# Steps of gathers and combines at three fixed places of a chunk, five weight pieces apart

## The chip, the cores and the metric

The kernel runs on one core of a Trainium2 chip. The metric is the device time of one execution in microseconds (us), from the first to the last instruction with what the device needs around it; the time shown for a kernel is the median of its runs. Engines: PE (TensorE) multiplies matrices, DVE (VectorE) and ACT (ScalarE) work on rows of data, POOL (GpSimd) and SP (SyncE) do little here beyond issuing transfers.

## The reference

A trunk of two layers on 256 tokens of width 1024. Each layer mixes tokens (attention and a linear recurrence) and then channels. The first layer's channel mixer is dense. The second layer's is a mixture of eight experts, two for each token, and it is the part that the change touches:

```python
def swiglu(h, wg, wu, wd):
    return (jax.nn.silu(h @ wg) * (h @ wu)) @ wd

def moe_swiglu(h2, router, wg, wu, wd):
    ...
    logits = jnp.matmul(h2, router, preferred_element_type=jnp.float32)
    top_logit, top_e = lax.top_k(logits, TOP_K)
    top_w = jax.nn.softmax(top_logit, axis=-1)
    ...
    yb = lax.map(expert_block, (xg.reshape(n_blocks, MOE_BLOCK, d), block_e)).reshape(n_rows, d)
    return jnp.zeros_like(h2).at[tok_buf].add(yb * w_buf[:, None].astype(h2.dtype), mode='drop')
```

So the rows of an expert's tokens are gathered, go through gate (1024 to 3584), up (1024 to 3584) and down (3584 to 1024), are weighted, and are added back to their tokens. All weights are float32.

## The kernel before

**Arithmetic.** A float32 weight tile is split into a high part `wh` (ACT, line 121) and the remainder `wl` (DVE, line 124). With both operands in two parts a product takes three matmuls (lines 133 to 135). A *piece* is 128 x 1024 weights: one `wh` and one `wl`. Weights come in transfers of 2 MB, four pieces each, issued by SP into six slots.

**Experts.** Slot r = 0 holds expert 0, slots 1 to 7 the others in order of their token count. Slots 0 to 3 are *long* (128 rows), slots 4 to 7 *short* (64 rows; both parts of the activations stand side by side in one operand, so two matmuls a product do, lines 902 and 903). In a short expert about one piece in six is not split but multiplied whole in float32 (line 898).

**Steps.** The 3584 columns of an expert are cut into chunks of 512; a step `(r, f0, m)` takes m = 2 chunks, or 1 where 512 are left. Long and short steps alternate: `(0,0,1) (0,512,2) (4,0,2) (0,1536,2) (4,1024,2) (0,2560,2) (4,2048,2) (1,0,2) (4,3072,1) (1,1024,2) (5,0,2)` and so on to `(7,2048,2) (7,3072,1)`. The loop does gate (4m pieces), up (4m pieces), and then the down (`down`, 4 pieces for each chunk) of the step *before*. In the gate it also does that earlier step's `turn`: PE transposes its activations, ACT and DVE split them.

**Order.** `take()` hands out pieces and keeps five in hand, so the split of piece p+4 stands in the queues of ACT and DVE ahead of whatever the code writes after piece p. `keep_order` fixes the written order on PE, DVE and ACT. So what the code writes between two pieces stands just there on PE, and four pieces later among the splits on DVE and ACT.

**Side work.** `dispatch(r)` gathers the rows of slot r: a mask P and its weighted twin C on DVE (lines 842, 843), two halves of 24 small matmuls on PE (line 826) with their evacuation by ACT and DVE, and `places` (two transposes of C, reduced to `wp` and `PT`). `combine` adds a finished expert back, in two halves of 512 columns: `yh` on ACT (line 946), `yl` on DVE (line 947), four matmuls on PE (lines 951, 952), two additions to `xk` on DVE (line 953). Both are generators that wait in the list `behind`; a call of `advance()` runs the first of them to its next `yield`. Before the change `advance()` stands after every second piece in the gate (places 3 and 5, where the turns take 0 and 1) and after every second piece in the down. At the start of an expert the rest is done at once:

```python
            if f0 == 0:
                settle()
```

Such a start follows seven times: at slots 4 (nothing is left there), 1, 5, 2, 6, 3 and 7. At the last six a `combine` has been put into `behind` by the `down` just before, so that all of it is done there, between the last product of that down and the first product of the next gate.

**Banks.** PSUM has eight banks, four tags of two: y0 and y1 collect the downs of the long and the short expert, "g" the gate, "u" the up. Before the change turns, gathers and combines all use "u".

Of the kernel before, what the change touches and what calls it, by code (L numbers as in the profile page):

```python
# [10 lines left out]
F32 = mybir.dt.float32  # L11
# [22 lines left out]
NLONG, SHORT, LEAD = 3, 64, 2  # L34
# [25 lines left out]
def trunk_kernel(ctx: ExitStack, tc: tile.TileContext, x, positions, norm1_g, w_in, q_norm_g, w_uq,  # L60
# [702 lines left out]
    def moe(l, norm, lgT):  # L763
# [10 lines left out]

        def bank(tag="u"):
            t = banks.tile([128, 512], F32, name="bk", tag=tag, bufs=2)
            return t
# [51 lines left out]
        def dispatch(r):  # L829
# [15 lines left out]
            for j0 in range(0, DB, 4):  # L845
                pg = bank()
                gather(pg, j0, P)
                v = pg.rearrange("p (j s) -> p j s", j=4)
                js = slice(j0, j0 + 4)
                if sh:  # L850
                    if j0 == 0:
                        A.activation(xw, v[:, :, :SHORT], AF.Copy)
                    A.activation(xa[:, js, :SHORT], v[:, :, :SHORT], AF.Copy)
                    V.tensor_sub(xa[:, js, SHORT:], v[:, :, SHORT:], f32(xa[:, js, :SHORT]))
                else:
                    split_act(xgh[:, js], xgl[:, js], v)
                yield
            xg[r] = (xa, xw) if sh else (xgh, xgl)
# [80 lines left out]

        def combine(y, wp, PT):  # L940

            for n in range(2):
# [6 lines left out]
                for t in range(2):  # L949
# [3 lines left out]
                    V.tensor_add(xk[:, t, c], xk[:, t, c], po)  # L953
                yield

        behind = []

        def advance():

            if behind and next(behind[0], "end") == "end":  # L960
                behind.pop(0)

        def settle():
            while behind:
                advance()

# [14 lines left out]
        def overflow_round():  # L981
            en = mp.tile([128, 1], F32, name="en")
            V.memset(en, 0.0)
            with tc.For_i(0, NE, 1) as e:
# [21 lines left out]
                for f0 in chunks:  # L1006
# [18 lines left out]
                    for b in range(4):  # L1025
                        for n in range(2):
                            PE.matmul(y[n], at[:, b], w[:, b, n * 512:(n + 1) * 512],
                                      start=f0 == 0 and b == 0, stop=f0 + CH == FE and b == 3)
                behind.append(combine(y, *rows))
                settle()  # L1030
# [157 lines left out]
        def take():  # L1188
            while len(ready) < len(pieces):
                p = next(supplies, None)  # L1190
                if p is None:
                    break
                ready.append(p)
            return ready.pop(0)

        y = {}

        def down(r, f0, m, acts):
            sh = is_short(r)
            if f0 == 0:  # L1200
                y[sh] = [bank(f"y{int(sh)}") for _ in range(2)]
            for p in range(4 * m):
                pc = take()
                for n in range(2):
                    products(y[sh][n], acts, p, pc, 0, slice(n * 512, (n + 1) * 512), f0 == 0 and p == 0,
                             f0 + m * CH == FE and p == 4 * m - 1)
                if p % 2:
                    advance()
            if f0 + m * CH == FE:
                behind.append(combine(y[sh], *back[r]))  # L1210

        behind.append(dispatch(NLONG + 1))
        prev, last = steps[0], (fc, P0)
        for r, f0, m in steps[1:]:
            sh = is_short(r)
            if f0 == 0:
                settle()
            x = xg[r]
            acts = acts_of(prev[0])
            pg = [bank("g") for _ in range(m)]  # L1220
            for w in range(2):
# [3 lines left out]
                for p in range(4 * m):  # L1225
                    pc = take()
                    for a in range(2 // m):
                        for n in range(m):
                            k = p if m == 2 else 2 * p + a
                            products((pu if w else pg)[n], x, k, pc, a, slice(n * CH, (n + 1) * CH), k == 0, k == DB - 1)  # L1230
                    if w == 0 and p < prev[2]:
                        turn(prev[0], last[0], p, acts, last[1])
                    elif w == 0 and p % 2 and p + 2 < 4 * m:
                        advance()
                if w == 0:
# [9 lines left out]
            if f0 + m * CH == FE:  # L1245
                after = r + 1 if r not in (NLONG, NE - 1) else None
                if after:
                    behind.append(dispatch(after))
            down(*prev, acts)
            prev, last = (r, f0, m), ((s, u) if sh else s, None)  # L1250

# [5 lines left out]
        for n in range(2):  # L1257
            for b, pc in enumerate(pcs):
                products(y[True][n], acts, b, pc, 0, slice(n * 512, (n + 1) * 512), False, b == 3)
            if n == 0:  # L1260
                behind.append(combine(y[True], *back[r]))
                advance()
        settle()
# [52 lines left out]
```

## Time and profile before

| what | value |
|---|---|
| median of 3 runs | 1558.34 us (1556.06 to 1560.99) |
| the profiled execution: its time / its span | 1555.83 us / 1554.1 us |
| PE busy | 1503.4 us (97% of the span) |
| DVE busy | 1269.7 us (82%) |
| ACT busy | 1019.3 us (66%) |
| weight transfers, q1 | 437.58 MB, 74.7% of 16 engines' span |
| granted TensorE clock, mean | 0.988 |

The mixture of experts is the last and longest part of the span, from about 575 us to its end. In the profile, a line such as L951 is a line of the kernel before. A matmul's duration contains the filling and emptying of the array, so two that follow each other overlap; how fast PE goes is read from the distance of their starts.

### The profile page before, as it was taken

The numbers are of one execution on the slowest core, as the hardware profiler recorded it, in microseconds if no ns is written. First come the engines' busy times: TensorE is split into PE (matmuls) and PEld (weight loads), VectorE is DVE, ScalarE is ACT, GpSimd is POOL, SyncE is SP. The second block draws the span as 40 slices with busy tenths as digits, with TensorE's granted clock in tenths as the row PEclk, the third lists the DMA queues.
The fourth block names the chain that finished last, engine by engine and source line by source line (L and its number), as shares of the span: only waits on it lengthen the run. The fifth ranks groups of instructions, "written<-read, shape, count | busy, mean of one in ns | idle before, by whom it ended". The sixth has DMA issues, their size and how long they took to land.

```text
span 1554.1 us, 22618 instructions
## 1 busy us (share of the span) xinstructions
PE 1503.4 (97%) x8624; PEld 1234.9 (79%) x8624; DVE 1269.7 (82%) x1787; ACT 1019.3 (66%) x1319; POOL 110.4 (7%) x133
## 2 busy tenths in 40 slices
PE   6999999999999999999999999999999999999996
PEld 5899999999899987867677677677676767767764
DVE  7986876657887898897978888878898888898985
ACT  4595454444596477776767777756677667677863
POOL 6210400004111400000000000000000000000000
PEclk9999999999999999999999999999999999999998
DMA  7329554441338639999979899989799989989990
GB/s 224 113 105 359 183 208 175 150 169 57 116 110 309 246 145 344 391 386 373 390 297 366 312 374 393 381 305 372 284 399 366 395 326 346 356 344 363 402 352 29
DMA packets 139701, 439.71 MB, mean 283 GB/s; under 512 B 5934, under 2 KB 12180, under 8 KB 139588
## 3 DMA queue, kind: packets, MB, share of 16 engines
q1 hardware_dynamic: 139284, 437.58, 74.7%
q8 instruction: 70, 1.15, 0.3%
q0 software_dynamic: 272, 0.62, 0.2%
q14 instruction: 43, 0.35, 0.1%
q10 hardware_dynamic: 32, 0.01, 0.0%
HBM read 437.15 MB, written 1.05 MB: 282 GB/s over the span
## 4 chain that ended last, share of the span: by engine, by line
PE 84%; DVE 11%; issue 2%; ACT 2%; POOL 1%; DMA 1%; SPq 0%; DVEq 0%; ACTq 0%; POOLq 0%
PE bk L133 18%; PE bk L134 18%; PE bk L135 18%; PE bk L902 8%; PE bk L903 7%; PE bk L898 6%; DVE wl L124 6%; PE bk L915 3%; PE bk L826 1%; PE bk L926 1%; PE bk L952 1%; ACT wh L121 1%; POOL nacc L307 1%; DVE yl L947 1%; PE bk L517 1%
## 5 line engine op out<-in xcount | busy, mean ns | idle before, releaser
L124 DVE TENSOR_TENSOR wl<-raw,wh 128x1024 fp32r<-128x1024 f32 x757 | 896.8, 1226 | 118.0 <-ACT wh L121 115.9
L121 ACT ACTIVATE wh<-raw 128x1024 fp32r<-128x1024 f32 x773 | 789.5, 1054 | 268.3 <-PE bk L134 141.5
L133 PE MATMUL bk<-hh,wh 128*128 128x256 f32 x800 | 232.9, 292 | 4.8 <-ACT hh L299 4.6
L134 PE MATMUL bk<-hlo,wh 128*128 128x256 f32 x800 | 228.3, 285 | 2.1 <-DVE hlo L300 2.1
L135 PE MATMUL bk<-hh,wl 128*128 128x256 f32 x800 | 227.5, 285 | 0.4 <-DVE wl L124 0.4
L133 PE MATMUL bk<-wh,xg 128*128 128x512 f32 x432 | 174.7, 404 | 0.0
L134 PE MATMUL bk<-wl,xg 128*128 128x512 f32 x432 | 171.8, 398 | 0.0
L135 PE MATMUL bk<-wh,xg 128*128 128x512 f32 x432 | 171.7, 398 | 0.0
L133 PEld LDWEIGHTS bk<-hh,wh 128*128 128x128 f32 x800 | 154.4, 193 | 7.2 <-ACT hh L299 5.0
L134 PEld LDWEIGHTS bk<-hlo,wh 128*128 128x128 f32 x800 | 154.5, 193 | 3.9 <-DVE hlo L300 2.5
L902 PE MATMUL bk<-wh,xa 128*128 128x512 f32 x392 | 157.5, 402 | 0.0
L135 PEld LDWEIGHTS bk<-hh,wl 128*128 128x128 f32 x800 | 154.2, 193 | 0.9 <-DVE wl L124 0.8
L903 PE MATMUL bk<-wl,xa 128*128 128x512 f32 x392 | 154.9, 395 | 0.0
L135 PEld LDWEIGHTS bk<-wh,xg 128*128 128x128 f32 x432 | 81.8, 189 | 19.7
L133 PEld LDWEIGHTS bk<-wh,xg 128*128 128x128 f32 x432 | 82.1, 190 | 18.3
L134 PEld LDWEIGHTS bk<-wl,xg 128*128 128x128 f32 x432 | 82.0, 190 | 18.3
L902 PEld LDWEIGHTS bk<-wh,xa 128*128 128x128 f32 x392 | 74.2, 189 | 27.5 <-ACT wh L121 6.5
L133 PE MATMUL bk<-wh,ax 128*128 128x512 f32 x224 | 89.1, 398 | 0.0
L134 PE MATMUL bk<-wl,ax 128*128 128x512 f32 x224 | 88.6, 395 | 0.0
L135 PE MATMUL bk<-wh,al 128*128 128x512 f32 x224 | 88.1, 394 | 0.0
L903 PEld LDWEIGHTS bk<-wl,xa 128*128 128x128 f32 x392 | 74.2, 189 | 16.2 <-DVE wl L124 0.6
L902 PE MATMUL bk<-wh,ax 128*128 128x512 f32 x170 | 71.7, 422 | 1.8 <-DVE ax L129 1.8
(351 smaller groups left out, 2278.2 us busy)
## 6 DMA issues: line engine op xcount, KB each, us to landing
raw<-in_moe_w_gate_dram SPq DMA_DIRECT2D x56, 2048.0 KB, 8.9
raw<-in_moe_w_up_dram SPq DMA_DIRECT2D x56, 2048.0 KB, 10.0
raw<-in_moe_w_down_dram SPq DMA_DIRECT2D x55, 2048.0 KB, 11.8
raw<-in_w_in_dram SPq DMA_DIRECT2D x12, 2048.0 KB, 7.8
raw<-in_ffn_w_gate_dram SPq DMA_DIRECT2D x5, 2048.0 KB, 9.1
raw<-in_ffn_w_up_dram SPq DMA_DIRECT2D x5, 2048.0 KB
raw<-in_ffn_w_down_dram SPq DMA_DIRECT2D x5, 2048.0 KB, 7.9
raw<-in_w_o_dram SPq DMA_DIRECT2D x4, 2048.0 KB
```

What stands on the lines that cost most here:

```text
L121: A.activation(hv, view, AF.Copy)
L124: eng.tensor_sub(lv, view, f32(hv))
L133: PE.matmul(o, l[0], r[0], start=start, stop=False, **kw)
L134: PE.matmul(o, l[0], r[1], start=False, stop=False, **kw)
L135: PE.matmul(o, l[1], r[0], start=False, stop=stop, **kw)
L307: G.tensor_add(self.acc, self.acc, sq)
L517: PE.matmul(ps[:, i], qT[:QD, h0 + i, t * 128:(t + 1) * 128], kT[:QD, h0 + i, :nk], start=True, stop=True)
L826: PE.matmul(pg[:, j * 128:(j + 1) * 128], xs[k][:, t, (j0 + j) * 128:(j0 + j + 1) * 128], P[:, t], start=k == 0 and t == 0, stop=k == 2 an ...
L898: PE.matmul(o[:SHORT], l[1][:, k], r[0][:, a, c], start=start, stop=stop)
L902: PE.matmul(o, l[0][:, k], r[0][:, a, c], start=start, stop=False)
L903: PE.matmul(o, l[0][:, k], r[1][:, a, c], start=False, stop=stop)
L915: PE.matmul(p4[:, k, b], s[k][:, (4 * h + b) * 128:(4 * h + b + 1) * 128], fold, start=True, stop=True)
```

## The change

`advance` gets a rule and the places of its calls are thinned out. A generator's next step runs only if at least five pieces have been taken since its last one (`met` counts them; `always=True` overrides it). The calls stand at three places: after piece 5 of an up of eight pieces, and after one or two given pieces of the down (1 and 4, or 2, or 3 and 4, by the sizes of the steps). Each call names the tag of banks, "g" or "u", that its step uses. `begin` runs a generator's first step at once when nothing else waits. `combine` loses the `yield` between a half's matmuls and the next half's `yh` and `yl`, so it has three steps; `dispatch` does both halves of its gather in one step. The `settle()` at an expert's start becomes a loop that only waits for that expert's own gather, and a new set `pending` makes a `down` settle if the accumulators that it starts on have not been emptied. In a gate of eight pieces the turns move from places 0 and 1 to 2 and 3. The rest of the arithmetic, the weights, the splits and the transfers are as they were. (A hunk in the code for an overflowing expert, which these inputs don't enter, is left out below.)

```diff
-        def bank(tag="u"):
-            t = banks.tile([128, 512], F32, name="bk", tag=tag, bufs=2)
+        aux = ["u"]
+
+        def bank(tag=None):
+            t = banks.tile([128, 512], F32, name="bk", tag=tag or aux[0], bufs=2)
             return t
...
                     split_act(xgh[:, js], xgl[:, js], v)
-                yield
+            yield
             xg[r] = (xa, xw) if sh else (xgh, xgl)
             back[r] = places(C, sh)
...
-        def combine(y, wp, PT):
+        def combine(y, wp, PT, kind=None):
...
                     V.tensor_add(xk[:, t, c], xk[:, t, c], po)
-                yield
-
-        behind = []
-
-        def advance():
-
-            if behind and next(behind[0], "end") == "end":
-                behind.pop(0)
+            pending.discard(kind)
+
+        pending = set()
...
+        behind, met = [], [0]
+
+        def advance(tag="u", always=False):
+            if behind and (always or met[0] - behind[0][1] >= len(pieces)):
+                g = behind.pop(0)[0]
+                aux[0] = tag
+                if next(g, "end") != "end":
+                    behind.insert(0, (g, met[0]))
+                aux[0] = "u"
+
+        def begin(g):
+            if not behind:
+                next(g)
+            behind.append((g, met[0]))
 
         def settle():
             while behind:
-                advance()
+                advance(always=True)
...
+            met[0] += 1
             return ready.pop(0)
...
-        def down(r, f0, m, acts):
+        def down(r, f0, m, acts, banks_at):
             sh = is_short(r)
             if f0 == 0:
+                if sh in pending:
+                    settle()
                 y[sh] = [bank(f"y{int(sh)}") for _ in range(2)]
...
-                if p % 2:
-                    advance()
+                if p in banks_at:
+                    advance(banks_at[p])
             if f0 + m * CH == FE:
-                behind.append(combine(y[sh], *back[r]))
-
-        behind.append(dispatch(NLONG + 1))
+                pending.add(sh)
+                begin(combine(y[sh], *back[r], sh))
+
+        begin(dispatch(NLONG + 1))
...
-            if f0 == 0:
-                settle()
+            while r not in back:
+                advance(always=True)
...
-                    if w == 0 and p < prev[2]:
-                        turn(prev[0], last[0], p, acts, last[1])
-                    elif w == 0 and p % 2 and p + 2 < 4 * m:
-                        advance()
+                    t = p - 2 * (m - 1)
+                    if w == 0 and 0 <= t < prev[2]:
+                        turn(prev[0], last[0], t, acts, last[1])
+                    elif w == 1 and m == 2 and p == 5:
+                        advance("g")
...
-                    behind.append(dispatch(after))
-            down(*prev, acts)
+                    begin(dispatch(after))
+            down(*prev, acts, {1: "g", 4: "u"} if m == 1 else {2: "g"} if prev[2] == 1 else {3: "g", 4: "u"})
...
             if n == 0:
-                behind.append(combine(y[True], *back[r]))
-                advance()
+                begin(combine(y[True], *back[r]))
```

Where the instructions went shows in three places. First PE, at the end of slot 4, the first short expert (`y` is its finished sum, `xa` the gathered rows of slot 5, whose gate follows; `ident,s` is a turn). Before, the eight products of the combine stand between the last down product and the first gate product:

```order
L902 MATMUL bk<-wh,ax 128x512
L903 MATMUL bk<-wl,ax 128x512
L951 MATMUL bk<-yh,PT 128x512
L952 MATMUL bk<-yl,PT 128x512
L951 MATMUL bk<-yh,PT 128x512
L952 MATMUL bk<-yl,PT 128x512
L951 MATMUL bk<-yh,PT 128x512
L952 MATMUL bk<-yl,PT 128x512
L951 MATMUL bk<-yh,PT 128x512
L952 MATMUL bk<-yl,PT 128x512
L902 MATMUL bk<-wh,xa 128x512
L903 MATMUL bk<-wl,xa 128x512
```

Now the gate follows the down at once, and this is where the first half of the same combine stands, after piece 5 of slot 5's up:

```order
L904 MATMUL bk<-wh,xa 128x512
L905 MATMUL bk<-wl,xa 128x512
L953 MATMUL bk<-yh,PT 128x512
L954 MATMUL bk<-yl,PT 128x512
L953 MATMUL bk<-yh,PT 128x512
L954 MATMUL bk<-yl,PT 128x512
L904 MATMUL bk<-wh,xa 128x512
L905 MATMUL bk<-wl,xa 128x512
```

The eight products were moved into the stream of weights, four after piece 5 of the up and four after piece 3 of the down behind it. Second DVE, from the same place on (`wl` is a split, `al` a turn, `s` the copy of the finished up). Before:

```order
L947 SCALAR_TENSOR_TENSOR yl<-bk,wp,yh 128x512
L953 TENSOR_TENSOR xk<-xk,bk 128x512 x2
L947 SCALAR_TENSOR_TENSOR yl<-bk,wp,yh 128x512
L953 TENSOR_TENSOR xk<-xk,bk 128x512 x2
L124 TENSOR_TENSOR wl<-raw,wh 128x1024
L129 TENSOR_TENSOR al<-bk,ax 128x512
L124 TENSOR_TENSOR wl<-raw,wh 128x1024
L129 TENSOR_TENSOR al<-bk,ax 128x512
L124 TENSOR_TENSOR wl<-raw,wh 128x1024 x13
L1242 COPY s<-bk 128x512 x2
```

After:

```order
L949 SCALAR_TENSOR_TENSOR yl<-bk,wp,yh 128x512
L124 TENSOR_TENSOR wl<-raw,wh 128x1024 x3
L129 TENSOR_TENSOR al<-bk,ax 128x512
L124 TENSOR_TENSOR wl<-raw,wh 128x1024
L129 TENSOR_TENSOR al<-bk,ax 128x512
L124 TENSOR_TENSOR wl<-raw,wh 128x1024 x9
L955 TENSOR_TENSOR xk<-xk,bk 128x512 x2
L949 SCALAR_TENSOR_TENSOR yl<-bk,wp,yh 128x512
L124 TENSOR_TENSOR wl<-raw,wh 128x1024 x2
L1261 COPY s<-bk 128x512 x2
L124 TENSOR_TENSOR wl<-raw,wh 128x1024 x4
L955 TENSOR_TENSOR xk<-xk,bk 128x512 x2
```

The additions and the second `yl` now stand among the splits, and the two turns stand two splits later. Third DVE at the gather of slot 5, in the down of slot 1's first step. Before:

```order
L1242 COPY s<-bk 128x512
L124 TENSOR_TENSOR wl<-raw,wh 128x1024 x2
L842 TENSOR_SCALAR P<-iota_6697,pos_r 128x128
L843 TENSOR_SCALAR C<-iota_6697,pos_r,wsel_r 128x128
L842 TENSOR_SCALAR P<-iota_6697,pos_r 128x128
L843 TENSOR_SCALAR C<-iota_6697,pos_r,wsel_r 128x128
L124 TENSOR_TENSOR wl<-raw,wh 128x1024 x2
L854 TENSOR_TENSOR xa<-bk,xa 128x4x64
```

After:

```order
L1261 COPY s<-bk 128x512
L844 TENSOR_SCALAR P<-iota_6697,pos_r 128x128
L845 TENSOR_SCALAR C<-iota_6697,pos_r,wsel_r 128x128
L844 TENSOR_SCALAR P<-iota_6697,pos_r 128x128
L845 TENSOR_SCALAR C<-iota_6697,pos_r,wsel_r 128x128
L124 TENSOR_TENSOR wl<-raw,wh 128x1024 x5
L856 TENSOR_TENSOR xa<-bk,xa 128x4x64 x2
```

P and C moved two splits up, and the evacuation of both halves of the gather stands together, five splits after them.

## Rows read from the trace of the kernel before

**Rows 1.** The page: busy time of the engines; the chain that ended last.
```profile
PE 1503.4 (97%) x8624; PEld 1234.9 (79%) x8624; DVE 1269.7 (82%) x1787; ACT 1019.3 (66%) x1319; POOL 110.4 (7%) x133
...
PE 84%; DVE 11%; issue 2%; ACT 2%; POOL 1%; DMA 1%; SPq 0%; DVEq 0%; ACTq 0%; POOLq 0%
```
**Rows 2.** Waits of PE from 575 to 1510 us: total us, times, longest.
```profile
PE bk L952 <- DVE yl L947: 10.7, 12, 2.7
PE bk L951 <- ACT yh L946: 4.8, 12, 0.6
PE bk L826 <- DVE P L842: 2.6, 6, 0.7
```
**Rows 3.** Six stretches: length, then busy us (instructions) by engine, PEclk, DMA share, GB/s.
```profile
767.02:775.26 8.24, 5.12 (x13) 3.01 (x12) 6.59 (x9) 2.32 (x4) 0.00 (x0) 0.79 1.02 406
863.61:870.79 7.18, 5.49 (x14) 3.23 (x13) 4.85 (x7) 2.29 (x3) 0.00 (x0) 0.76 0.74 287
1013.66:1024.58 10.92, 7.23 (x17) 4.37 (x15) 8.44 (x10) 2.30 (x4) 0.00 (x0) 0.69 1.03 403
1112.27:1119.23 6.96, 5.27 (x14) 3.02 (x13) 4.84 (x7) 2.29 (x3) 0.00 (x0) 0.81 0.75 294
1262.45:1273.17 10.72, 7.04 (x16) 4.19 (x15) 8.42 (x10) 2.30 (x4) 0.00 (x0) 0.70 1.03 404
1361.09:1365.92 4.83, 3.14 (x10) 1.53 (x9) 2.96 (x5) 2.29 (x3) 0.00 (x0) 1.00 1.00 383
```
**Rows 4.** Timeline of PE at slot 1's end: start, us, operation, idle before.
```profile
1008.30 0.39 PE L133 MATMUL bk<-wh,ax 128*128 128x512 f32 x1
...
1013.66 0.40 PE L135 MATMUL bk<-wh,al 128*128 128x512 f32 x1
...
1017.61 0.80 PE L952 MATMUL bk<-yl,PT 128*128 128x512 f32 x1 [2.72 <-DVE yl L947]
```
**Rows 5.** Timeline of DVE in slot 5's first gate, up and the down behind.
```profile
872.08 0.69 DVE L129 TENSOR_TENSOR al<-bk,ax 128x512 fp32r<-128x512 f32 x1 [0.93 <-ACT ax L128]
873.02 1.22 DVE L124 TENSOR_TENSOR wl<-raw,wh 128x1024 fp32r<-128x1024 f32 x1 [0.25 <-ACT wh L121]
874.53 0.69 DVE L129 TENSOR_TENSOR al<-bk,ax 128x512 fp32r<-128x512 f32 x1 [0.28 <-ACT ax L128]
875.47 14.88 DVE L124 TENSOR_TENSOR wl<-raw,wh 128x1024 fp32r<-128x1024 f32 x13 [0.25 <-ACT wh L121]
890.27 1.28 DVE L1242 COPY s<-bk 128x512 f32<-128x512 f32 x2
```
**Rows 6.** Timeline of PE there: up's first piece, down's third, each where `wl` is read.
```profile
879.43 0.39 PE L903 MATMUL bk<-wl,xa 128*128 128x512 f32 x1
...
890.69 0.40 PE L134 MATMUL bk<-wl,ax 128*128 128x512 f32 x1
```
**Rows 7.** Groups of DVE from 575 us on: busy us, mean ns, idle before.
```profile
L953 DVE TENSOR_TENSOR xk<-xk,bk 128x512 f32<-128x512 f32 x32 | 21.2, 684 | 12.2 <-PE bk L952 12.2
...
L947 DVE SCALAR_TENSOR_TENSOR yl<-bk,wp,yh 128x512 fp32r<-128x512 f32 x16 | 11.9, 744 | 7.6 <-ACT yh L946 7.6
```
**Rows 8.** Timeline of PE at slot 5's gather.
```profile
824.84 0.40 PE L135 MATMUL bk<-wh,al 128*128 128x512 f32 x1
825.86 0.23 PE L826 MATMUL bk<-P,xs 128*128 128x128 bf16 x1 [0.62 <-DVE P L842]
826.30 1.44 PE L826 MATMUL bk<-P,xs 128*128 128x128 bf16 x23 [0.22 <-DVE P L842]
```
**Rows 9.** Timeline of DVE there: first mask, next split.
```profile
825.52 0.28 DVE L842 TENSOR_SCALAR P<-iota,pos_r 128x128 bf16<-128x128 f32 x1
...
826.43 2.35 DVE L124 TENSOR_TENSOR wl<-raw,wh 128x1024 fp32r<-128x1024 f32 x2
```
**Rows 10.** Timeline of PE at the end: the last turn.
```profile
1533.45 2.00 PE L915 MATMUL bk<-fold,s 128*128 128x64 f32 x16 [1.90 <-DVE xk L953]
```
**Rows 11.** What the queue of weight transfers waits for, longest.
```profile
SPq L875 <- DVE wl L124: 458.8, 103, 16.9
```

More of the change, by code (lines that the diff above doesn't have):

```diff
@@ L1028, in overflow_round @@
                                       start=f0 == 0 and b == 0, stop=f0 + CH == FE and b == 3)
-                behind.append(combine(y, *rows))
+                begin(combine(y, *rows))
                 settle()
```

## The prediction

> **What bounds the kernel now.** I read the page first: PE is busy for 97% of the span and makes 84% of the chain that ended last [rows 1]. So a change in order can give only what PE loses. Next I read PE's waits in the mixture of experts: it waits for a combine's `yl` and `yh` and for a gather's mask P, and for no split and no transfer [rows 2]. Then I looked at where these waits fall. Six stretches, each the start of an expert where `settle()` runs a whole combine, hold nearly all of the first two [rows 3]. Each is cut from the start of the last product of the down to the start of the first work of the next gate that PE does at full speed again. There the reader is to see three things: the length, the number of matmuls, and PEclk below 1 in five of the six.
>
> At full speed 24 products in a row start within 1013.66 - 1008.30 = 5.36 us [rows 4], 23 distances of 0.233 us. The sharpest single loss is 2.72 us, where PE stands for `yl` [rows 4]: DVE had four splits in its queue ahead of it.
>
> **The change part by part.** *The settles go.* Of the matmuls in rows 3 one (in the third, two) only overlaps an edge; 12, 13, 15, 13, 15 and 9 start inside. Eight of them are the combine, which is done elsewhere after the change, and the others are products that stay. At 0.233 us each they need 2.80, 3.03, 3.50, 3.03, 3.50 and 2.10 us. The lengths are 8.24, 7.18, 10.92, 6.96, 10.72 and 4.83 us, so the losses are 5.44, 4.15, 7.42, 3.93, 7.22 and 2.73: together **30.9 us**, from waits and from the low clock behind them. After the change the gate follows the down at once, and its first pieces are split already, since five are always in hand. The bounds on this term come from the clock: the share of clock withheld times the length is 1.7, 1.7, 3.4, 1.3, 3.2 and 0, or 11.3 us in all [rows 3]. If none of this were there to regain, 19.6 us would be left; if the sixth stretch (same waits as the second and fourth, full clock) lost clock like these, it would be 32.3.
>
> In this case's rows the clock is at the full 2.4 GHz before each settle and at 1.2 GHz in part of five of them, after PE had stood still, while the sixth, with standstills too, kept it. The Trainium skill, page "TensorE: Matmul & The Clock Gate", section "Part 1: The HAM clock gate", says that the default state is throttled, that activity releases it, and that where the change falls differs from run to run. The sixth row agrees. By the rule the clock's part of the gain is a matter of luck in each run; by the rows it was there five times of six, and I keep it whole.
>
> *The combine moves into the stream.* Its eight products cost PE the same 1.86 us there as here. What is new lies on DVE: two additions and one `yl`, 2 x 0.684 + 0.744 = 2.1 us [rows 7], stand among the splits at the first half, 1.4 us at the second, and everything behind them is late by that. Queued behind are the splits of the down's third piece and on, and PE waits for those if the lead is gone. In the three starts of *long* experts (slots 1, 2, 3) there is room: a piece is six products, 1.40 us, on PE, and a split is 1.145 us on DVE (14.88 / 13) [rows 5], so each piece adds 0.25 us to the lead, and two turns of a short step add PE work. I take 0 there.
>
> The starts of *short* experts (5, 6, 7) are the thin place: a split piece takes PE only 0.93 us. In slot 5's first up, the first piece's `wl` is the third of the 13 splits [rows 5], done at 875.47 + 3 x 1.145 + 0.07 = 878.97; PE reads it at 879.43 [rows 6]: 0.46 us in hand. The change alters this lead four ways. The turns stand two splits later, so that DVE no longer stands 0.93 + 0.25 + 0.28 = 1.46 us behind them [rows 5]. DVE and ACT begin the gate about 0.5 us later against PE, as PE doesn't wait for their `yh` and `yl`. PE no longer runs the first matmuls at half speed, which gave 1.0 us. Together: about 0.4 us in hand at the up's first piece. For the down's third piece, the twelfth split ends at 889.28 at the latest and is read at 890.69 [rows 5, 6]: 1.4 in hand. After: 1.4 + 1.46 - 0.5 - 1.0 - 2.1 (additions and `yl`) + 0.93 (four products of the combine on PE) = 0.2 us. Behind that the copies of `s` (1.28 us [rows 5]) come just as before, and the second half gives 0.93 and takes 1.4. So the lead stays near zero without a clear wait. I allow 0.3 us for each of the three: **0.9 us** lost. The bounds are 0, and 2 x 2.1 - 2 x 0.93 = 2.3 us each if the lead were gone from the start.
>
> *The gathers.* At three of them PE stands for P: the first matmul should start at 824.84 + 0.23 = 825.07 and starts at 825.86; the next one starts 0.44 us on where 0.06 is usual [rows 8]. Less 0.08 for the change of operation that any gather pays, that is 0.79 - 0.08 + 0.38 = 1.1 us, and 3.3 for three. Now P and C are made at the begin of the down, five pieces ahead of the gather. They take DVE 0.91 us (825.52 to 826.43) [rows 9] before the split of the down's fifth piece, where two splits stood between before, so I allow 0.15 us there. Gain **3.3 - 0.5 = 2.8 us**. The other gathers cost the same; joining their halves saves one change of operation each, which I leave out. `places` moves to piece 5 of an up: PE's two transposes and DVE's two short operations trade places with equal work, taken at 0.
>
> *The end.* The last turn waits 1.90 us for the additions of slot 3's second half [rows 10]. In the changed order one of two `yl` is done much earlier, in the last gate, where DVE waits for turns; so DVE is early by 0.74 [rows 7]: **0.7 us**, between 0 and 1.9. The very last combine is as it was.
>
> *Transfers.* SP issues a transfer when a slot comes free, and what it waits for is DVE, not the memory [rows 11]. A faster PE frees slots earlier. In the second and fourth stretch the DMA share is 0.74 and 0.75 [rows 3]: there is capacity left where the stalls go. I take 0.
>
> **Sum.** 30.9 - 0.9 + 2.8 + 0.7 = **33.5 us**. The profiled execution took 1555.83 us (its span 1554.1), so it would take 1522.3. It lies 2.5 us under the median of 1558.34; the losses are in every run, so I take the sum from the median: 1558.34 - 33.5 = 1524.8, or **1525 us**.
>
> **The rivals.** *Part is given back in the short experts.* DVE is 82% busy over the span, and every settle also let it catch up. If the lead is at zero from the first placed step on, the three short starts cost 2.3 us each and a clock loss of about 1.5 each (the second and fourth stretch against the sixth) [rows 3]: 11.4 instead of 0.9, and 1535. If the long ones did the same, 23 and 1547. Against it: the lead of 0.2 to 0.4 that the rows give, and that a long step follows. For it: how thin that lead is. Beyond 1538 I give it 0.08.
>
> *Slower than before.* The mechanism is one wait in place of another: at each of the twelve placed halves PE would stand for `yl` as at slot 1's end, 2.72 us [rows 4], and lose half of 3.4 us of clock [rows 3] behind it: 4.4 x 12 = 53 us against 33.5 gained, hence 1578. It decides from 33.5 / 12 = 2.8 us a half on. Against it: at a placed half `yl` was queued five pieces before, 4.6 us of short products, and PE reaches it later than ever before; for it, that ACT and DVE take their work in order and now wait for PE in the middle of a stage. Chance 0.06. The Trainium skill, page "PSUM — Partial Sum Buffer", section "Engine vs sequencer instructions", says that these two engines' queues are strictly first in, first out. By that rule an addition that waits for PE holds up every split behind it, which is this rival's lever; no row here shows it apart from the order that the program wrote.
>
> *No change.* If the weights' transfers set the pace, removing stalls would only move them to the splits: 1558. For it: DMA shares of 1.02 and 1.03 in three stretches [rows 3]. Against it: no wait of PE for a transfer or a split [rows 2], and rows 11. That the change doesn't do what it says is excluded by the order, where the eight products are gone from the settle. Chance 0.04.
>
> **How the numbers follow.** The forecast has 0.82. Its range: at the low end nothing new is lost (1.4), the end gives all (1.2) and the sixth stretch's clock is lost too (1.4): 33.5 + 4.0 = 37.5, hence 1521, and 1518 with the scatter of some 2.5 us that the three runs show. At the high end the clock's 11.3 us are not regained: 33.5 - 11.3 = 22.2, hence 1536, and 1538 with scatter. The rivals lie above. Faster by over 0.3% (4.7 us, about what a measurement can tell from no change): 0.82 + 0.08 = 0.90; within: 0.04; slower: 0.06.
>
> **What would show it.** In the new profile: no combine between a down and the next gate, and no PEclk below 0.95 from 600 us to 1500 us. PE's waits for `yl`, `yh` and P from 575 to 1480 us fall from 18 us to under 2. The span falls by about as much as rows 3 lose. New waits, if any, would be for `wl`, in the down behind slots 5, 6 and 7's first gate and up. The forecast is wrong if PE waits there for over 1 us each, if the additions' line has a PE product waiting behind it in the gate of the next step (the "g" banks), or if a wait for a transfer appears.

## The result

The changed kernel takes 1523.44 us (median of 4 runs, 1522.75 to 1525.18), the kernel before, in runs beside it, 1559.66 us. The ratio is 0.9772, 95% interval 0.975 to 0.9794: some 36 us faster. The forecast was 1525 us. The profiled execution took 1522.75 us, where the sum made against the profiled execution of before said 1522.3.

In the profile, line numbers from the combine on are those of the changed kernel: `yh` and `yl` are L948 and L949 (before L946 and L947), their products L953 and L954 (L951, L952), the additions L955 (L953), a short expert's products L904 and L905 (L902, L903). The page first, as in [rows 1]: busy time of the engines, and the chain that ended last.

```profile
PE 1487.3 (98%) x8624; PEld 1229.0 (81%) x8624; DVE 1266.6 (83%) x1787; ACT 1017.9 (67%) x1319; POOL 110.4 (7%) x133
...
PE 90%; DVE 6%; ACT 1%; POOL 1%; issue 1%; DMA 1%; SPq 0%; DVEq 0%; ACTq 0%; POOLq 0%
```

PE runs the same 8624 matmuls in 16 us less busy time: a product counts as busy for 0.80 us in a settle ([rows 4]) and for 0.40 in the stream. DVE's part of the chain fell from 11% to 6%. Next PE's waits from 575 to 1490 us. There is one row (what waits, for whom: us in total, times, longest):

```profile
PE bk L935 <- DVE xg L129: 1.0, 1, 1.0
```

The 18 us of [rows 2] are gone. Three long windows of the changed kernel (columns as in [rows 3]) show PE without a gap and the clock at its upper level; where [rows 3] had PEclk 0.69 to 0.81 nothing is left to see:

```profile
600.00:900.00 300.00, 300.00 (x1387) 226.42 (x1387) 267.93 (x275) 223.28 (x251) 0.00 (x0) 1.00 0.96 372
900.00:1200.00 300.00, 300.00 (x1374) 223.88 (x1373) 265.11 (x272) 222.79 (x253) 0.00 (x0) 1.00 0.97 374
1200.00:1475.00 275.00, 275.00 (x1247) 202.85 (x1246) 244.69 (x250) 204.51 (x232) 0.00 (x0) 1.00 0.98 375
```

To compare kernels closely I use two lengths read from each trace: the **stretch**, from the first product of the gate of step (0,512,2) to the first product of the down of step (7,2048,2), and the **end**, from there to the end of the span. What differs ahead of them is scatter of stages that no kernel here changes (1.3 us between these two profiles, up to 5.2 among all eleven).

| kernel | median us | ratio to before (95%) | stretch | end |
|---|---|---|---|---|
| before | 1559.66 | | 946.8 | 35.0 |
| changed | 1523.44 | 0.9772 (0.975 to 0.9794) | 913.2 | 34.3 |
| e1 settle back | 1552.67 | 0.9964 (0.9948 to 0.998) | 943.6 | 34.9 |
| e2 settle gone, else before | 1533.44 | 0.9838 (0.982 to 0.9855) | 921.2 | 35.8 |
| e3 spacing 1 | 1525.92 | 0.9784 (0.9768 to 0.9801) | 917.4 | 31.4 |
| e4 turns early | 1524.09 | 0.9778 (0.9762 to 0.9795) | 912.4 | 35.1 |
| e5 before, clock kept | 1548.92 | 0.9933 (0.9917 to 0.9948) | 938.1 | 34.6 |
| e6 last turn in the down | 1518.04 | 0.9729 (0.971 to 0.9748) | 913.1 | 27.3 |
| e7 additions doubled | 1535.71 | 0.9849 (0.9829 to 0.9868) | 921.5 | 37.4 |
| e8 old places | 1526.37 | 0.9785 (0.9772 to 0.9799) | 917.8 | 33.8 |
| e9 e6 and early turns | 1516.73 | 0.9725 (0.9712 to 0.9739) | 912.4 | 27.6 |

So the change gained 33.7 us in the stretch and 0.7 at the end, 34.4 together. The two profiled spans differ by 33.1, because the 1.3 us of scatter ahead of the stretch go the other way; without them the sum's 33.5 would be 0.9 off, and not 0.4.

### The profile page after: what moved, and what is told of

Same layout as the page of the kernel before. It is cut to its first block, busy times and chain, and to the rows that moved or that the text cites. A ratio compares the mean times of both kernels' runs of the same rounds, so it can differ in the third digit from the quotient of the medians.

```text
span 1521.0 us, 22641 instructions
## 1 busy us (share of the span) xinstructions
PE 1487.3 (98%) x8624; PEld 1229.0 (81%) x8624; DVE 1266.6 (83%) x1787; ACT 1017.9 (67%) x1319; POOL 110.4 (7%) x133
## 4 chain that ended last, share of the span: by engine, by line
PE 90%; DVE 6%; ACT 1%; POOL 1%; issue 1%; DMA 1%; SPq 0%; DVEq 0%; ACTq 0%; POOLq 0%
PE bk L133 19%; PE bk L134 19%; PE bk L135 19%; PE bk L904 9%; PE bk L905 8%; PE bk L900 6%; PE bk L917 3%; DVE wl L124 2%; PE bk L828 1%; PE bk L928 1%; POOL nacc L307 1%; PE bk L517 1%; PE bk L540 1%; DMA raw<-in_w_in_dram 1%; PE bk L954 0%
## 5 line engine op out<-in xcount | busy, mean ns | idle before, releaser
L904 PE MATMUL bk<-wh,xa 128*128 128x512 f32 x392 | 158.6, 405 | 0.0
L905 PE MATMUL bk<-wl,xa 128*128 128x512 f32 x392 | 154.0, 393 | 0.0
L904 PEld LDWEIGHTS bk<-wh,xa 128*128 128x128 f32 x392 | 73.6, 188 | 34.0 <-ACT wh L121 13.0
L905 PEld LDWEIGHTS bk<-wl,xa 128*128 128x128 f32 x392 | 73.7, 188 | 14.8 <-DVE wl L124 0.2
L904 PE MATMUL bk<-wh,ax 128*128 128x512 f32 x170 | 71.4, 420 | 1.8 <-DVE ax L129 1.8
## 6 DMA issues: line engine op xcount, KB each, us to landing
raw<-in_moe_w_down_dram SPq DMA_DIRECT2D x55, 2048.0 KB, 10.8
```

Of the source, the lines that this page charges most:

```text
L904: PE.matmul(o, l[0][:, k], r[0][:, a, c], start=start, stop=False)
L905: PE.matmul(o, l[0][:, k], r[1][:, a, c], start=False, stop=stop)
```

## The experiments

### Is the settle the loss? (e1)

The changed kernel with the settle back at every expert's start:

```diff
-            while r not in back:
-                advance(always=True)
+            if f0 == 0:
+                settle()
```

> The changed kernel with one thing undone: at the start of every expert the whole of what is left behind is settled again, as before the change. Spacing and places stay. If the six settles are the loss, their six combines come back between a down and the next gate, PE waits there for yl and yh for some 15 us in all and the clock falls behind five of them: 1523.4 plus about 28 to 31 us, so 1551 to 1555. If instead the gain came from the spacing and from the places in gate and up, most of it stays and the time is 1530 or less.

1552.67 us. The stretch is 30.4 us longer than the changed kernel's, against 30.9 in the prediction. PE's waits from 575 to 1480 us are those of [rows 2] again, without the ones for P:

```profile
PE bk L954 <- DVE yl L949: 11.0, 12, 2.9
PE bk L953 <- ACT yh L948: 4.8, 12, 0.6
```

The settle is the loss; the other explanation, that spacing and places alone made the gain, falls. This trace also tells something on the clock. Here are two of its settles, before a short expert and before a long one (columns as in [rows 3]):

```profile
868.99:873.84 4.85, 3.15 (x11) 1.53 (x10) 3.40 (x6) 3.24 (x4) 0.00 (x0) 1.00 0.99 372
...
1017.65:1028.58 10.93, 7.01 (x16) 4.17 (x15) 8.65 (x11) 2.30 (x4) 0.00 (x0) 0.71 1.03 404
```

All three settles before short experts kept the full clock here (4.85, 4.84 and 4.83 us long), with the same waits with which two of three lost it in the kernel before (7.18 and 6.96 us [rows 3]). Before the long experts it fell in three of three, in both kernels. So the sum of 30.4 is nearer to the prediction than its parts are: less nine products of 0.233 us each, the short settles lose 8.2 us here against 10.8 in [rows 3], and if all the rest is the long ones', these lose 22.2 against 20.1. (Behind the first of them the low clock lasted longer: it was 0.72 in the mean of 771.48 to 783.00 us.) That the two differences nearly cancel is chance.

### How much of it is the clock? (e5)

The kernel before, with matmuls that nothing reads where PE stands in the six settles. They multiply an `xs` tile into a free "g" bank:

```diff
+        def fill(k):
+            d = bank("g")
+            for _ in range(k):
+                PE.matmul(d, xs[0][:, 0, :128], xs[0][:, 0, :512], start=True, stop=True)
...
                     po = bank()
+                    if filling and t == 0:
+                        fill(filling[0][n][0])
                     PE.matmul(po, PT[:, t], yh, start=True, stop=False)
+                    if filling and t == 0:
+                        fill(filling[0][n][1])
...
             if f0 == 0:
+                filling.append(((1, 1), (2, 2)) if sh else ((1, 8), (2, 2)))
                 settle()
+                filling.pop()
```

> The kernel before, with matmuls added whose results nothing reads, only in the six settles at an expert's start: PE works on them where it stood for yh and yl (9 and 4 of 512 columns at the two halves before a long expert, 2 and 4 before a short one, 0.23 us each). The waits themselves are as long as before. If the clock falls because PE stood still there, the granted clock of the six stretches stays at or near 1 and the part of their length that the low clock cost comes back: up to 11.3 us by the clock's shares, some 7 to 9 us where the products behind also run early, so 1550 to 1553. If the clock falls for another reason, the time is that of the kernel before, 1558 to 1560, and the shares stay at 0.7 to 0.8.

1548.92 us, 11 us less by the medians and a little under the 1550 to 1553 that were expected. The six settles, cut as in [rows 3], from the last product of the down to the first of the gate (same columns):

```profile
768.63:774.96 6.33, 5.80 (x23) 2.56 (x23) 5.15 (x8) 2.32 (x4) 0.00 (x0) 1.00 1.03 411
864.01:868.84 4.83, 4.27 (x15) 1.95 (x15) 2.95 (x5) 2.30 (x3) 0.00 (x0) 1.00 0.98 376
1012.62:1019.91 7.29, 5.95 (x23) 2.56 (x22) 6.10 (x8) 2.30 (x4) 0.00 (x0) 1.00 1.03 410
1108.99:1113.83 4.84, 4.30 (x16) 1.96 (x16) 2.97 (x5) 2.30 (x3) 0.00 (x0) 1.00 0.95 365
1257.58:1264.86 7.28, 5.97 (x22) 2.56 (x22) 6.09 (x8) 2.29 (x4) 0.00 (x0) 1.00 1.03 410
1353.98:1358.82 4.84, 4.28 (x16) 1.96 (x16) 2.96 (x5) 2.29 (x3) 0.00 (x0) 1.00 0.93 377
```

PEclk is 1.00 in all six, where five were below. Nine of the matmuls in each are useful ones (the last product and the combine's eight), 2.10 us at 0.233; so the losses are 4.23, 2.73, 5.19, 2.74, 5.18 and 2.74, together 22.8 us instead of 30.9. **The clock was 8.1 us of the settles' loss, PE standing still (with the changes of operation) 22.8.** The stretch is 8.7 us shorter, the medians say 11, with an interval of about 8 to 13.

What PE works on is of no matter to the clock in these rows. The Trainium skill, page "TensorE: Matmul & The Clock Gate", section "Part 1: The HAM clock gate", says that the throttled state is the default and activity releases it, and that where the change falls varies. The traces agree in part: with useless matmuls in the waits the clock stayed up in six settles of six, and the settles before short experts fell on either side (e1 against [rows 3]). Before long experts nothing varied, and the clock fell six times of six.

### Is the removed settle enough? (e2)

The kernel before with only the settle gone. The places stay at every second piece, with no spacing:

```diff
-            if f0 == 0:
-                settle()
+            while r not in back:
+                advance()
```

> The kernel before with one part of the change alone: the settle at an expert's start is gone, and only a gather that is still due is finished there. The combines then advance at the old places, after every second piece, so that yl is queued two pieces ahead of its products, behind splits that DVE holds already. If the spacing of five pieces is needed too, PE waits for yl inside the downs, about 1.5 to 3 us a combine behind the short starts (2 pieces of 0.93 us against four splits of 1.15 us) and 0 to 1 behind the long ones, clock included some 8 to 15 us in all, and the three gathers' 3.3 us stay: 1535 to 1545. If taking the settle away is all of the gain but the gathers, 1527.

1533.44 us, 25 us of the 36, and a little under the 1535 to 1545 that were expected. The stretch is 8.1 us longer than in the changed kernel. PE's waits from 575 to 1480 us:

```profile
PE bk L952 <- DVE yl L947: 4.4, 6, 0.8
PE bk L826 <- DVE P L842: 2.6, 6, 0.7
```

One of the six, first in PE's timeline (start, us, engine, operation; idle before in brackets):

```profile
870.68 0.40 PE L951 MATMUL bk<-yh,PT 128*128 128x512 f32 x1
871.84 0.50 PE L952 MATMUL bk<-yl,PT 128*128 128x512 f32 x1 [0.77 <-DVE yl L947]
```

And in DVE's timeline of the same kernel:

```profile
868.76 2.36 DVE L124 TENSOR_TENSOR wl<-raw,wh 128x1024 fp32r<-128x1024 f32 x2 [0.25 <-ACT wh L121]
871.04 0.74 DVE L947 SCALAR_TENSOR_TENSOR yl<-bk,wp,yh 128x512 fp32r<-128x512 f32 x1
```

DVE comes to `yl` at 871.04, behind two splits that it could begin only behind the turns; PE was there at 870.68. All six waits are behind the short starts, two for each, and the clock stayed at its upper level around them (granted 1.00 in seven us around each), where the expectation had some clock loss. With the change of operation behind them they cost about 1.0 us each, 6.0 in all; the gathers, with the waits of [rows 2], cost about 2.5 more than in the changed kernel. So the settle is the most of it, and the remaining 8 us are the new order's.

### Distance or place? (e3 and e8)

e3 keeps the three places and lets the steps be one piece apart. e8 keeps five pieces and puts the places and banks back (the turns stay at 2 and 3, so that the places in a gate of eight pieces behind a step of two chunks are 1 and 5, not 3 and 5):

```diff
-            if behind and (always or met[0] - behind[0][1] >= len(pieces)):
+            if behind and (always or met[0] - behind[0][1] >= 1):
```
```diff
-                    elif w == 1 and m == 2 and p == 5:
-                        advance("g")
+                    elif w == 0 and p % 2 and p + 2 < 4 * m:
+                        advance()
...
-            down(*prev, acts, {1: "g", 4: "u"} if m == 1 else {2: "g"} if prev[2] == 1 else {3: "g", 4: "u"})
+            down(*prev, acts, {p: "u" for p in range(1, 8, 2)})
```

> The changed kernel with the steps one piece apart at least, in place of five; the places stay, so a gather runs at the first place that comes after its masks are asked for, and yh and yl are made right before or one or two pieces ahead of their products. If the distance is what hides the masks and yl, PE waits for P again at each gather (1.1 us each, as before the change, for three to six of them) and for yl: 1523.4 plus 5 to 12 us, so 1528 to 1535. If the places alone hide them, 1523.4 within 0.2%.

> The changed kernel with the spacing of five pieces kept and the places put back where they were before the change: every second piece of a gate and of a down, always in up's free banks. It is the other half of the run with a spacing of one. If the distance in pieces is what hides yl and the masks, PE has no wait for yl or P from 575 to 1480 us and the time is 1523 to 1527. If the three places and the idle banks are needed, PE waits for a bank or for wl at the steps that fall elsewhere, 0.5 to 1 us at each of twelve halves: 1530 to 1536.

e3: 1525.92 us, not to be told from the changed kernel by time. That lies within the 0.2% that were expected if the places alone hide everything, but for another reason: the stretch is 4.3 us longer, and the end 2.9 shorter, because slot 3's second half is done earlier and the last turn no longer waits for its additions. What lengthens the stretch is one wait, and it is not `yl`:

```profile
PE bk L828 <- DVE P L844: 4.2, 6, 1.2
```

The masks are made right before the gather again, behind six splits and a copy, and PE comes to the gather two pieces earlier than before the change, so that it stands longer than in [rows 8]: 1.15 and 0.24 us. In e3's timeline of DVE:

```profile
813.99 7.02 DVE L124 TENSOR_TENSOR wl<-raw,wh 128x1024 fp32r<-128x1024 f32 x6 [0.25 <-ACT wh L121]
820.92 0.69 DVE L1261 COPY s<-bk 128x512 f32<-128x512 f32 x1
821.52 0.28 DVE L844 TENSOR_SCALAR P<-iota,pos_r 128x128 bf16<-128x128 f32 x1
```

And PE beside it:

```profile
821.85 0.22 PE L828 MATMUL bk<-P,xs 128*128 128x128 bf16 x1 [1.15 <-DVE P L844]
822.31 0.89 PE L828 MATMUL bk<-P,xs 128*128 128x128 bf16 x13 [0.24 <-DVE P L844]
```

e8: 1526.37 us, stretch 4.6 us longer. No wait for `yl`, none for P, but a new one, at each of the three short starts:

```profile
PE bk L953 <- DVE s L1261: 3.2, 3, 1.1
```

The first of them in PE's timeline:

```profile
880.53 0.50 PE L953 MATMUL bk<-yh,PT 128*128 128x512 f32 x1 [1.08 <-DVE s L1261]
```

The step fell on the down's second piece, where both "u" banks still held the up's result and DVE had three splits to do ahead of the copies that empty them when PE ended the up, at 876.5. Of the expectation for a gain by distance alone the time came true, and so did its claim of no waits for `yl` and P; the wait for a bank, which the other one named, came too, at three halves and not at twelve. **Taken together:** only the distance hides the masks (4.2 us), and only the places and the idle banks keep PE from a full bank (some 4.5 us). For `yl` either is enough on top of what both runs share. They share something that e2 lacks too: `begin`, which has the first `yl` made right behind the expert's last down, and the merged steps. No run takes these out alone, so their part in hiding `yl` is not shown.

### What sets the lead at the short starts? (e4 and e7)

e4 puts the turns back at the first two pieces of a gate. e7 has DVE copy each bank onto itself ahead of the addition, work that nothing needs:

```diff
-                    t = p - 2 * (m - 1)
+                    t = p
```
```diff
+                    if kind is not None:
+                        V.tensor_copy(po, po)
                     V.tensor_add(xk[:, t, c], xk[:, t, c], po)
```

> The changed kernel with the turns back at the first two pieces of a gate, two pieces earlier, where DVE stood 1.46 us behind them. The up's first piece of a short start has its wl 0.5 us before PE reads it in the changed kernel. If that lead is as thin as the sum of the prediction had it, PE waits about 1 us at each of the three short starts, for wl of the up or of the down: about 1526 to 1527, seen as new waits for wl of 2 to 3 us in sum. If the lead is set elsewhere: 1523.4 and no wait for wl.

> The changed kernel with the work of DVE at each of the combines' additions about doubled: the bank is first copied onto itself (about 0.7 us each, four for a combine). This measures what DVE work among the splits costs. If DVE has room in the downs behind long starts and none to speak of behind short ones, as the prediction's leads of 0 and 0.2 to 0.5 us say, the three long ones cost nothing, the three short ones up to 2 x 1.4 us less 0.5 each, and the end 1.4: about 8 us, so 1531. If DVE sets the pace everywhere, all 28 copies count: 19 us and 1542. If there is room everywhere, only the end's 1.4: 1525.

e4: 1524.09 us, no wait for `wl` anywhere, the stretch 0.8 us *shorter*. Of its two expectations the second came true, that the lead is set elsewhere. These are DVE's rows at slot 5's start in the changed kernel (they answer [rows 5]):

```profile
864.41 0.69 DVE L129 TENSOR_TENSOR al<-bk,ax 128x512 fp32r<-128x512 f32 x1 [0.26 <-ACT ax L128]
865.36 1.23 DVE L124 TENSOR_TENSOR wl<-raw,wh 128x1024 fp32r<-128x1024 f32 x1 [0.26 <-ACT wh L121]
866.50 0.68 DVE L129 TENSOR_TENSOR al<-bk,ax 128x512 fp32r<-128x512 f32 x1
867.10 10.40 DVE L124 TENSOR_TENSOR wl<-raw,wh 128x1024 fp32r<-128x1024 f32 x9
877.42 1.28 DVE L955 TENSOR_TENSOR xk<-xk,bk 128x512 f32<-128x512 f32 x2
878.62 0.74 DVE L949 SCALAR_TENSOR_TENSOR yl<-bk,wp,yh 128x512 fp32r<-128x512 f32 x1
879.28 2.35 DVE L124 TENSOR_TENSOR wl<-raw,wh 128x1024 fp32r<-128x1024 f32 x2
```

PE reads the `wl` of the up's first piece and of the down's third here:

```profile
868.83 0.39 PE L905 MATMUL bk<-wl,xa 128*128 128x512 f32 x1
...
881.03 0.40 PE L134 MATMUL bk<-wl,ax 128*128 128x512 f32 x1
```

The same place in e4:

```profile
864.87 0.69 DVE L129 TENSOR_TENSOR al<-bk,ax 128x512 fp32r<-128x512 f32 x1 [0.25 <-ACT ax L128]
865.82 12.61 DVE L124 TENSOR_TENSOR wl<-raw,wh 128x1024 fp32r<-128x1024 f32 x11 [0.26 <-ACT wh L121]
```

In the changed kernel the run of splits behind the turns begins with the up's first piece, in e4 two pieces earlier, just as before the change. Yet `wl` of that first piece is done 0.51 us before PE reads it in the changed kernel, 0.46 in e4 and 0.46 before the change. At the down's third piece it is 0.53 in the changed kernel and 0.55 in e4. So neither the turns' place nor what happened ahead of them sets this lead. The rows fit this reading: DVE waits for PE (through ACT) at the turns, and from there the lead begins anew.

Two runs made for other questions bear it out. e1 has the settle in front of the same gate, with the turns where the changed kernel has them; its run of splits and PE's read of the first of them are

```profile
881.70 12.67 DVE L124 TENSOR_TENSOR wl<-raw,wh 128x1024 fp32r<-128x1024 f32 x11
...
883.43 0.39 PE L905 MATMUL bk<-wl,xa 128*128 128x512 f32 x1
```

PE reads 1.73 us after the run's start, as in the changed kernel (868.83 - 867.10): a lead of 0.51 with a settle ahead and without one. e5 has the order of before, but no low clock ahead of the turns:

```profile
874.42 14.88 DVE L124 TENSOR_TENSOR wl<-raw,wh 128x1024 fp32r<-128x1024 f32 x13 [0.25 <-ACT wh L121]
...
878.38 0.39 PE L903 MATMUL bk<-wl,xa 128*128 128x512 f32 x1
```

Here it is 3.96 us, as in the kernel before (879.43 - 875.47 [rows 5, 6]): a lead of 0.46 with the low clock ahead and without it.

e7: 1535.71 us, more than expected, but where expected. The stretch is 8.3 us longer. PE's only new wait from 575 to 1480 us is for `wl`, twice behind each of the three short starts:

```profile
PE bk L134 <- DVE wl L124: 5.6, 6, 1.1
```

There PE loses 2.46 us (1.09 at the down's third piece, 1.37 at the next gate's first), with the change of operation behind the wait; behind a long start it loses 0.3. By the trace, half of the miss is in the stretch, where some 7 us were expected; the other half is at the end, 3.1 us instead of 1.4: the last turn waits 3.94 us, and then runs itself at the low clock (granted 0.51), 3.68 us instead of 2.00.

```profile
1510.62 3.68 PE L917 MATMUL bk<-fold,s 128*128 128x64 f32 x16 [3.94 <-DVE xk L957]
```

DVE doesn't set the pace everywhere (28 copies of 0.7 us are 19 us, and 11.4 came out). But behind short starts the room is what the lead says, half a microsecond.

### Beyond the change: the last turn (e6, e9)

In the changed kernel the end still has what [rows 10] showed. The last turn waits for additions in front of it, and the products behind it for the turn (timeline of PE):

```profile
1500.40 2.00 PE L917 MATMUL bk<-fold,s 128*128 128x64 f32 x16 [1.74 <-DVE xk L955]
1504.23 0.79 PE L904 MATMUL bk<-wh,ax 128*128 128x512 f32 x1 [1.84 <-DVE ax L129]
1504.82 0.63 PE L905 MATMUL bk<-wl,ax 128*128 128x512 f32 x1
```

e6 does that turn behind the fifth piece of the down ahead of it, into tiles of its own:

```diff
                 if p in banks_at:
                     advance(banks_at[p])
+                if within and p == 4:
+                    within()
...
-        acts = acts_of(r)
-        turn(r, last[0], 0, acts)
+        acts = ends
```

e9 also puts the turns of all steps early, as e4 did.

> The changed kernel with its last turn, the one of the last short step, put behind the fifth piece of the down before it, with tiles of its own for what it makes, so that the last four products' input is there when the additions of slot 3's second half are made. In the changed kernel PE stands 1.74 and 1.84 us around that turn and then runs 13 products at half speed, 2.5 us. If those waits are on the path, the end is 3 to 6 us shorter: 1517.5 to 1520.5. If the last additions or the last transfer set the end whatever PE does, 1523.4.

> The kernel with the last turn in the last down (1518.0 in its own run), and besides with the turns of every step at the first two pieces of a gate. The turns alone gave 912.4 in place of 913.2 us from the first gate to the last down, and cost that much again at the end, where the last turn is no longer: 1516.5 to 1518 if the gain of 0.8 us is real, 1518 to 1519 if it is scatter.

e6: 1518.04 us; the end is 7.0 us shorter, where 3 to 6 were expected. The turn stands in PE's stream without a wait, and the last four pieces follow the combine at full clock:

```profile
1495.16 1.89 PE L917 MATMUL bk<-fold,s 128*128 128x64 f32 x16
...
1501.50 0.40 PE L954 MATMUL bk<-yl,PT 128*128 128x512 f32 x1
1501.73 0.39 PE L904 MATMUL bk<-wh,xe 128*128 128x512 f32 x1
```

e9: 1516.73 us. Its stretch of 912.4 repeats e4's, so the early turns' 0.8 us are in two traces, one execution each; by time e9 is not to be told from e6 (their intervals overlap). Both beat the changed kernel, whose interval begins above theirs.

## Why the prediction was right, and where it was not

**What bounds the kernel:** right. PE's own stream, and what it lost at six places. With the losses gone PE has no gap for 875 us.

**The settles, 30.9 us:** right; 30.4 by e1, though there the shares of short and long settles are others and cancel by chance. The bound on the clock's part (11.3) was a true bound; its size was 8.1 (e5). Keeping it whole was right for the sum, since the waits of any length are gone. The Trainium skill, page "TensorE: Matmul & The Clock Gate", section "Part 1: The HAM clock gate", says that where the clock changes varies from run to run. That held for the three settles before short experts; before the long ones the runs show a fall each time.

**The short starts, 0.9 us lost:** the one step that failed, with little effect. Measured: no wait, and leads of 0.51 and 0.53 where 0.4 and 0.2 were forecast. Three terms of that lead (1.46 gained by the later turns, 0.5 lost by the earlier begin, 1.0 lost with the half speed) do not exist: e4 takes the first back, e1 the second, e5 has the third alone, and the lead moves by 0.05 at most. They cancelled to 0.04 by chance, so that the forecast of no clear wait was luck in this part. The remaining terms were right but for a duration. The additions and `yl` take 879.28 - 877.42 = 1.86 us from start to start, not 2.1, since the summed durations of neighbours on DVE overlap. From the 1.47 us that the trace of before has at this piece: 1.47 - 1.86 + 0.93 = 0.54, measured 0.53. The bound of 2.3 us for each start if the lead were gone was not tested: e7 loses 2.46, but with 2.8 us of DVE work that the sum did not have.

**The long starts, 0:** right, and e7 shows some room left there (0.3 us lost to 2.9 us more work).

**The gathers, 2.8 us:** nearly. No wait for P is left. But at the down's fifth piece PE loses 0.26 us at each of the three, not 0.15, so 2.5. One thing was left out: both halves of the first gather are now done in one go, so that its `places` waits 0.95 us instead of 0.42 for DVE's last split of it. Of the 33.7 us of the stretch, 30.9 + 2.5 - 0.5 = 32.9 are so accounted for. The other 0.8 is not traced; changes of operation saved in small places, which the prediction left out, may be in it.

**The end, 0.7 us:** right in size, 0.7; the wait for the last turn itself fell only from 1.90 to 1.74, and most of the rest is the wait for `yl` in front of it (0.20 us, and the change of operation behind it), which is gone.

**Transfers, 0:** right. PE waits for none of them, though their share of the 16 engines is 0.96 to 0.98 in the three long windows, where it was 0.93 and 0.94 before the change.

**The rivals.** A part given back in short experts did not come, though e7 shows that 0.7 us more for each addition would have brought most of it (8.3 us in the stretch). The wait of 2.72 us at each half did not come: that was the price of a settle. With neither distance nor places, nor `begin` (e2), a half waits 0.67 to 0.80 us, and only six of twelve do. The third rival, no change because the transfers set the pace, fell with the first row of waits.

## What to carry to other kernels

A "finish all of it here" call between two dense stretches costs the whole chain through three engines, and where its waits pull the clock down, the work behind pays too; cut it into steps of which each finds its input made some pieces ago. Distance (an input queued early enough) and place (a bank that is free there) fail in different ways, and the traces tell them apart by what is waited for. Before a lead between engines is carried through a sum, look for the last point ahead at which the faster engine waits for the slower: in these traces the lead began there, and what lay ahead of that point did not count.

## What the hardware showed that I had not expected

Matmuls that nothing reads kept the granted clock at 1.00 through six settles, of which five had a drop before, and were worth 8.1 us in a kernel whose combines they left where they were. The same standstills (0.33, 0.29, 0.55 and 0.53 us within 4.8 us) went with the low clock in two of three settles of one kernel and in none of three of another. And two neighbouring additions on DVE take 1.28 us together, where the mean of one is 0.684 [rows 7], so that a row's mean times a count is too much by some 7%.
